# A convolution layer's second projection by seven block products instead of eight, with sums made by adding DMA transfers

## The chip, the cores and the metric

The kernel runs on one core of a Trainium2 chip. The metric is the device time in microseconds (us) of one execution. The chip's TensorE is called PE in what follows, VectorE DVE, ScalarE ACT, GpSimd POOL and SyncE SP, as in the profile's pages; PEld is PE's loading of weights. SP and POOL issue the DMA transfers of the part that matters here.

## The reference

Two decoder layers on x of 1024 tokens by 1024 channels, all in float32. Layer 0 has a short convolution as its token mixer, layer 1 attention in a window of 128; each is followed by a SwiGLU channel mixer.

```python
def short_conv_mixer(h, w_in, conv_w, w_out):
    b_gate, c_gate, xv = jnp.split(h @ w_in, 3, axis=-1)
    u = b_gate * xv
    y = lax.conv_general_dilated(u, conv_w[:, None, :], ...)   # causal, width 3, one filter per channel
    return (c_gate * y) @ w_out                                 # the second projection: 1024 x 1024

def swiglu_ffn(h, w_gate_up, w_down):
    g, u = jnp.split(h @ w_gate_up, 2, axis=-1)
    return (jax.nn.silu(g) * u) @ w_down

for i in range(2):
    h = rmsnorm(x, norm_mixer[i])
    x = x + (short_conv_mixer(h, ...) if i == 0 else swa_sink_attention(h, ...))
    h = rmsnorm(x, norm_ffn[i])
    x = x + swiglu_ffn(h, w_gate_up[i], w_down[i])
```

## The kernel before

Everything is kept transposed: a tile `X0` to `X7` holds 128 channels by 1024 tokens, and a half of it (`lo_half`, `hi_half`) is 512 tokens. To keep float32 accuracy every operand and every weight is split into a high and a low part, `hi` (a cast on ACT) and `lo` (the rest, by a subtraction on DVE, `split_steps`). One product of a 128x128 weight block with 512 tokens is then three matmuls: hi by hi, hi by lo, lo by hi.

Most of the large products are block products of two by two blocks with seven products in place of eight (a Winograd form). The four operand blocks are an even and an odd channel tile, each by the two halves of the tokens. Seven sums of operands (kinds `k` = 0 to 6, `put` splits them) meet seven sums of weights. One product of such a kind, called a unit here, goes over four pairs of channel tiles: 4 x 3 = 12 matmuls. Results of several kinds accumulate in one PSUM bank (`acc`, four of them, or `P0`, `P1`).

Four of the seven weight operands are sums of weight blocks. `sums_in_place`, `store_sums` and `weight_sums` make them: SP loads raw blocks, DVE adds and subtracts, POOL stores the sums to DRAM, and SP loads them again when a unit wants them. The operand sums (T1 to T4, `sum_t1` to `sum_t4`) are made by DVE as well.

The second projection `w_out` of the convolution does not work so before. It is the "tail" of `channel_mixer`: for each half `h` and each of the eight output tiles `m`, `tail_item` runs 8 x 3 = 24 matmuls over the eight tiles `z` of the gated convolution (`split_z`), with weights that `tail_weights` loads and splits. Then DVE adds the residual tile `X[m]`, which `load_again` has fetched from DRAM, ACT squares the result, POOL stores it (`xres`), and DVE adds the square to the running sum `s0` or `s1` (`L1054`, `L1058`). While the tail runs, weights of the channel mixer's first three kinds are loaded, split and kept (`early`), and its weight sums are made.

When a half is complete, `half_chain` follows: PE sums the squares over the channels (`mean`, L1071), DVE and ACT make the inverse root (`guess`), and PE turns it into rows (`turn`, L1083). DVE then multiplies the eight tiles by gain and rows (`scale`, L1093), and `put` splits them into the channel mixer's operands.

The order on every engine is written out by hand. A `Line` has work on PE, one piece behind another, each matmul counted as 0.2265 (`MM`), and `at(t, f)` issues `f` on its engine just ahead of the PE work that stands at time `t` of that plan. Each engine runs its queue in that order, so an instruction that has to wait holds up all that stand behind it on its engine. A granule of weights (`ring_granule`) is planned so: its load 20 us ahead of its matmuls, its hi 13 us, its lo 12.2 us ahead. Eight buffers `G` form the ring for split weights, `WR` and `WH` hold raw ones.

In the plan, `s` is the place at which `lead_in` begins: there the convolution's last unit products and the second projection meet. `begin1` and `begin2` are the ends of the projection's first and second half.

Of the kernel before, what the change touches and what calls it, by code (L numbers as in the profile page):

```python
# [83 lines left out]
def trunk_kernel(ctx: ExitStack, tc: tile.TileContext, xT, small, w_in, w_out, w_qk, w_v, w_o, w_gu, w_dn, out):  # L84
# [212 lines left out]
    def conv_layer():  # L297
# [80 lines left out]

        at(-7.6, mean)
# [126 lines left out]
        def gate(j, h, src):  # L506
            c = halves[h]
            dve.tensor_tensor(Y[j][:, c], src(), Y[j][:, c], ALU.mult)
# [163 lines left out]
        def gate_back(j, name):  # L672
            dve.tensor_tensor(Y[j], R[name], Y[j], ALU.mult)
# [13 lines left out]
        z = [None] * NK  # L687

        def split_z(j, tag, h, t):
            it = {}  # L690

            def hi():
                if z[j] is None:
                    z[j] = pair_slot(tag)
                it["steps"] = split_steps(z[j][:, 0, halves[h]], z[j][:, 1, halves[h]], Y[j][:, halves[h]])
                it["steps"][0]()

            at(t, hi)
            at(t + 0.7, lambda: it["steps"][1]())

        def load_again(m, t):
            def load():
                X[m] = slot(f"X{m}")
                load_x(m)

            at(t, load)

        def lead_in(part):
            u = n_units - 1
            s = line.end  # L710
            for k in (2, 5, 3):
                steady(u, k)
            part(0, 0, range(4))
            steady(u, 4)
            part(0, 1, range(4))
            steady(u, 6)
            tags = ("A0", "A1", "A2", "A3", "A4", "A5", "XS4", "XS5")
            e = line.end - s
            low = (-6.5, -5.5, 0.2, 1.2, 5.6, 6.6, 8.6, e - 2 * unit + 0.8)
            high = (-1.5, 8.0, 10.0, e - 1.0, e + 4.0, e + 9.0, e + 14.0, e + 19.0)  # L720
            again = (1.0, 10.0, 12.0, e + 3.5, e + 7.0, e + 12.0, e + 17.0, e + 22.0)
            for j in range(NK):
                split_z(j, tags[j], 0, s + low[j])
                split_z(j, tags[j], 1, s + high[j])
                load_again(j, s + again[j])
            return {(0, 0): 4, (0, 1): 4}
# [4 lines left out]
            lambda m: w_out[m],  # L731
            z,
            raw_tags=("XS0", "XS1", "XS2", "XS3"),
            extra_tags=("XS6", "XS7"),
            keep_tags=None,
            line=line,
            lead_in=lead_in,
            slots=(
# [10 lines left out]

    xres = [tc.dram_tile((P, T), F32, name=f"xres{m}") for m in range(NK)]  # L750
    first_sums = [[tc.dram_tile((4, P, 4 * P), F32, name=f"s1_{l}_{u}") for u in range(GROUP)] for l in range(2)]
    down_sums = [[tc.dram_tile((4, P, PAIRS * P), F32, name=f"s2_{l}_{u}") for u in range(GROUP)] for l in range(2)]
# [41 lines left out]
    def weight_sums(dst, w1, w2, j0, n, raw_tag, sum_tag, line=None, t=0.0):  # L794

        c = slice(j0 * P, (j0 + n) * P)
        it = {}

        def load():
            raw = slot(raw_tag, (P, 2, 2, 2 * P), bufs=2 if raw_tag == "WL" else 1)[:, :, :, 0 : n * P]  # L800
            nc.sync.dma_start(raw[:, 0], w1[:, :, c])
            nc.sync.dma_start(raw[:, 1], w2[:, :, c])
            it["raw"] = raw

        def add():
            raw = it["raw"]
            s = it["s"] = slot(sum_tag, (P, 4, 2 * P), bufs=2 if sum_tag == "WL" else 1)[:, :, 0 : n * P]
            for f in sums_of(raw[:, 0, 0], raw[:, 0, 1], raw[:, 1, 0], raw[:, 1, 1], s[:, 3], s[:, 0], s[:, 2], s[:, 1]):
                f()

        def store():
            nc.gpsimd.dma_start(dst[:, :, c].rearrange("s p c -> p s c"), it["s"])

        if line is None:
            load()
            add()
            store()
        else:
            line.at(t, load)
            line.at(t + 7.0, add)  # L820
            line.at(t + 9.5, store)
# [27 lines left out]
    def scheme(line, ring_tags):  # L849
# [22 lines left out]
        ring = deque(ring_tags)  # L872
# [5 lines left out]
        raws = {"n": 0}  # L878
# [48 lines left out]
        def bank_at(u, name, tag):  # L927
# [10 lines left out]
            ring=ring,  # L938
            ring_room=ring_room,
# [7 lines left out]
    def operands_of(line, slots):  # L947

        B = {k: [] for k in range(KINDS)}

        def put(k, p, src, t, lo_eng=dve):
            it = {}

            def hi():
# [3 lines left out]
                it["steps"] = split_steps(o[:, 0, :], o[:, 1, :], src(), lo_eng)  # L958
# [7 lines left out]
    def channel_mixer(layer, next_stage, src_of, operands, raw_tags, extra_tags, keep_tags, slots, begin_with=(), first_w=None, line=None, lead_in=None):  # L966
# [9 lines left out]
        tools = scheme(line, [f"G{(3 + i) % RING}" for i in range(RING)])  # L976
# [62 lines left out]

        def tail_item(h, m, k0=0):  # L1040
# [3 lines left out]
            t = line.end  # L1044

            def square():
                if m == 0:
# [6 lines left out]
            at(t + 0.05, lambda: dve.tensor_tensor(X[m][:, c], get(), X[m][:, c], ALU.add))  # L1054
            at(t + 0.8, square)
            at(t + 0.9, lambda: nc.gpsimd.dma_start(xres[m][:, c], X[m][:, c]))
            if m:
# [37 lines left out]
        first_items = {}  # L1095
        if lead_in is not None:
            first_items = lead_in(tail_part)
        origin = line.end - sum(first_items.values()) * 3 * MM
        begin1 = origin + 8 * tail
        begin2 = origin + 16 * tail  # L1100
        for h in (0, 1):
            for m in range(NK):
                tail_item(h, m, first_items.get((h, m), 0))
# [3 lines left out]
        extra_rooms = rooms(extra_tags)  # L1107
        pairs = [{} for u in range(GROUP)]
        whole = len(raw_tags) == GROUP

        def first_raw(u, k):
            if k < 2:
                return pairs[u]["raw"][:, 0, k]
            return pairs[u]["raw"][:, 1, 1] if whole else pairs[0]["s2"][:, u]
# [7 lines left out]
        def load_s2():  # L1122
            pairs[0]["s2"] = slot(raw_tags[0], (P, 4, 4 * P))
            for u in range(GROUP):
                nc.sync.dma_start(pairs[0]["s2"][:, u], first_sums[layer][u][SUMS[2]])


        for u in range(GROUP):
            if whole:
                t = (origin + 4.0, origin + 12.0, begin1 + 1.0, begin1 + 8.0)[u]  # L1130
                at(t, load_pair, pairs[u], raw_tags[u], w_gu[layer, u], w_gu[layer, NF + u])
                ts = (t + 8.0, t + 10.0, t + 18.0)
                at(t + 12.0, sums_in_place, pairs[u], 0)
                at(t + 14.0, sums_in_place, pairs[u], 2)
                at(t + 15.5, store_sums, pairs[u], first_sums[layer][u])
            else:
                at(origin + 1.0 + u, load_first, u)
                ts = [origin + 8 * tail * f for f in (0.28 + 0.14 * u, 0.35 + 0.14 * u, 0.9 + 0.07 * u)]
            for k in range(3):
                split_granule(early[k, u], lambda u=u, k=k: first_raw(u, k), 4, extra_rooms[u] if k == 2 else ring_room, ts[k])  # L1140
# [1013 lines left out]
```

## Time and profile before

| | |
|---|---|
| median of three runs | 1940.71 us (1940.19 to 1941.73) |
| profiled execution | 1941.99 us, of which its span is 1940.0 us |
| PE, PEld, busy | 1933.7 us (100%), 1617.8 us (83%) |
| DVE, ACT, POOL busy | 1363.7 us (70%), 864.8 us (45%), 247.4 us (13%) |
| granted PE clock | 0.999 |
| DMA | 311.75 MB, mean 161 GB/s |

The span runs from the first instruction to the last, and the time of an execution has about 2 us around it. Busy shares are means over stages that differ; what an engine waits for is read from the views of the trace. A matmul's busy time overlaps with that of the next, so PE's pace is read from the starts of its matmuls.

### The profile page before, as it was taken

How to read it: one execution, taken by the hardware profiler on the slowest of the kernel's cores; microseconds unless marked ns; L12 is line 12 of the kernel's file. 1: busy time of each engine (PE TensorE's matmuls, PEld its weight loads, DVE VectorE, ACT ScalarE, POOL GpSimd, SP SyncE). 2: the span in 40 equal slices, each digit the busy share in tenths (PEclk: the TensorE clock that was granted, in tenths of full speed). 3: DMA queues.
4: the chain of work that ended last, by engine and by line, in shares of the span. 5: the costliest groups of instructions: out<-in, count | busy, mean ns of one | idle time of the engine just before them, and what ended most of it. 6: DMA issues, size and time to landing. Idle time of an engine off the chain costs nothing.

```text
span 1940.0 us, 25506 instructions
## 1 busy us (share of the span) xinstructions
PE 1933.7 (100%) x9153; PEld 1617.8 (83%) x9153; DVE 1363.7 (70%) x2432; ACT 864.8 (45%) x1702; POOL 247.4 (13%) x350
## 2 busy tenths in 40 slices
PE   9999999999999999999999999999999999999999
PEld 7888888888888888888898888888888888888887
DVE  8998767876777676765744777788677766775543
ACT  5543434523333335444435887656233333344441
POOL 0000011011111110000003445310111111110000
PEclk9999999999999999999999999999999999999999
DMA  8532285244565448976300000152455455378562
GB/s 320 162 98 88 65 305 183 82 158 174 184 202 177 175 159 284 332 268 200 119 23 23 23 12 17 37 192 63 161 195 183 171 199 179 134 272 288 190 231 101
DMA packets 143167, 311.75 MB, mean 161 GB/s; under 512 B 13888, under 2 KB 53952, under 8 KB 143040
## 3 DMA queue, kind: packets, MB, share of 16 engines
q1 hardware_dynamic: 118992, 225.67, 35.3%
q0 software_dynamic: 23904, 84.42, 11.2%
q8 instruction: 72, 1.18, 0.3%
q14 instruction: 55, 0.45, 0.1%
q10 hardware_dynamic: 144, 0.03, 0.0%
HBM read 219.36 MB, written 90.70 MB: 160 GB/s over the span
## 4 chain that ended last, share of the span: by engine, by line
PE 96%; DVE 2%; DMA 1%; issue 1%; ACT 0%; DVEq 0%; ACTq 0%
PE acc L906 15%; PE acc L909 15%; PE acc L907 15%; PE P L906 9%; PE P L907 9%; PE P L909 9%; PE acc L167 7%; PE acc L171 3%; PE acc L1036 2%; PE acc L1034 2%; PE acc L1035 2%; PE P L1779 1%; PE P L1603 1%; PE P L1804 1%; PE P L1805 1%; PE P L1737 1%
## 5 line engine op out<-in xcount | busy, mean ns | idle before, releaser
L906 PE MATMUL acc<-XS,G 128*128 128x512 f32 x894 | 348.2, 389 | 0.0
L909 PE MATMUL acc<-XS,G 128*128 128x512 f32 x894 | 347.8, 389 | 0.0
L907 PE MATMUL acc<-XS,G 128*128 128x512 f32 x894 | 347.8, 389 | 0.0
L909 PEld LDWEIGHTS acc<-XS,G 128*128 128x128 f32 x894 | 167.8, 188 | 34.9
L907 PEld LDWEIGHTS acc<-XS,G 128*128 128x128 f32 x894 | 167.8, 188 | 34.8
L906 PEld LDWEIGHTS acc<-XS,G 128*128 128x128 f32 x894 | 167.8, 188 | 34.8
L906 PE MATMUL P<-A,G 128*128 128x512 f32 x502 | 195.3, 389 | 0.0
L907 PE MATMUL P<-A,G 128*128 128x512 f32 x502 | 195.3, 389 | 0.0
L909 PE MATMUL P<-A,G 128*128 128x512 f32 x502 | 195.3, 389 | 0.0
L906 PE MATMUL acc<-A,G 128*128 128x512 f32 x410 | 159.5, 389 | 0.0
L907 PE MATMUL acc<-A,G 128*128 128x512 f32 x410 | 159.5, 389 | 0.0
L909 PE MATMUL acc<-A,G 128*128 128x512 f32 x410 | 159.5, 389 | 0.0
L846 DVE TENSOR_TENSOR G<-WL,G 128x512 fp32r<-128x512 f32 x168 | 115.0, 685 | 52.9 <-ACT G L845 52.9
L167 PE MATMUL acc<-XS,WH 128*128 128x512 f32 x480 | 148.6, 409 | 0.8 <-ACT WH L139 0.7
L845 ACT CAST G<-WR 128x512 fp32r<-128x512 f32 (+1 forms) x198 | 119.6, 604 | 63.3 <-PE acc L909 25.6
L846 DVE TENSOR_TENSOR G<-WR,G 128x512 fp32r<-128x512 f32 (+1 forms) x198 | 132.0, 667 | 10.9 <-ACT G L845 10.6
L845 ACT CAST G<-WH 128x512 fp32r<-128x512 f32 (+1 forms) x156 | 93.7, 600 | 81.5 <-PE acc L909 42.1
L1206 ACT ACTIVATE G<-G 128x512 f32<-128x512 f32 x88 | 55.7, 634 | 161.7 <-DVE G L1277 157.6
L845 ACT CAST G<-WL 128x512 fp32r<-128x512 f32 x168 | 103.6, 616 | 37.0 <-DVE WL L789 33.2
L906 PE MATMUL P<-XS,G 128*128 128x512 f32 x290 | 112.9, 389 | 0.1
L909 PE MATMUL P<-XS,G 128*128 128x512 f32 x290 | 112.8, 389 | 0.0
L907 PE MATMUL P<-XS,G 128*128 128x512 f32 x290 | 112.8, 389 | 0.0
(320 smaller groups left out, 3884.2 us busy)
## 6 DMA issues: line engine op xcount, KB each, us to landing
G<-h SPq DMA_DIRECT2D x70, 512.0 KB, 5.3
h<-X POOLq DMA_DIRECT2D x44, 512.0 KB, 5.7
X<-in_w_dn SPq DMA_DIRECT2D x80, 256.0 KB, 3.5
s<-X POOLq DMA_DIRECT2D x40, 512.0 KB, 4.5
WR<-in_w_gu SPq DMA_DIRECT2D x36, 512.0 KB, 5.7
WH<-in_w_gu SPq DMA_DIRECT2D x36, 512.0 KB, 6.1
h<-X POOLq DMA_DIRECT2D x66, 256.0 KB, 4.3
WR<-s SPq DMA_DIRECT2D x52, 256.0 KB, 3.3
```

Of the source, the lines that this page charges most:

```text
L167: pe.matmul(ps.half(h), wh, xs[:, j, c], start=first and j == 0, stop=False)
L171: pe.matmul(ps.half(h), wl, xs[:, 0, c], start=False, stop=last)
L845: lambda: act.copy(out_hi, raw),
L846: lambda: lo_eng.tensor_tensor(out_lo, raw, plain(out_hi), ALU.subtract),
L906: pe.matmul(ps, w[:, 0, c], x[:, 0, :], start=start and e == 0, stop=False, skip_group_check=True)
L907: pe.matmul(ps, w[:, 0, c], x[:, 1, :], start=False, stop=False, skip_group_check=True)
L909: pe.matmul(ps, w[:, 1, c], x[:, 0, :], start=False, stop=last, skip_group_check=True)
L1034: pe.matmul(ps, hi[:, kc], xs[:, 0, c], start=k == 0, stop=False, skip_group_check=True)
L1035: pe.matmul(ps, hi[:, kc], xs[:, 1, c], start=False, stop=False, skip_group_check=True)
L1036: pe.matmul(ps, lo[:, kc], xs[:, 0, c], start=False, stop=k == n_op - 1, skip_group_check=True)
L1206: state["silu"] = act.activation(x, x, AF.Silu)
L1603: pe.transpose(pb[:, t], wide[:, t], ident)
```

## The change

The second projection now uses the seven products too. `out_product(u, k)` is a unit of 12 matmuls for a pair of output tiles `u` (four pairs), so 7 x 4 units take the place of 2 x 8 items; the weights go through the ring. `lead_in` orders everything around it. Kinds 0 and 1 and kinds 2 to 4 of the units share a bank, and results are added to `X[m]` with the sign that the kind asks for.

Three kinds of sums are made by DMA transfers that add to what their target holds (`accum_op=ALU.add`, issued by POOL): the weight sums (`added_sums`: SP copies the four blocks from DRAM to DRAM, then POOL issues four adding transfers) for `w_out`, for the channel mixers' first group and for `w_down`; the operand sums of z for three of the four pairs of tiles (`add_by_dma`; the fourth is added by DVE, `add_here`); and the residual for three quarters of the output (`copy_out`: ACT copies the bank to `X[m]`, POOL adds x from DRAM to it). For transfers can only add, the signs of the operands change: some are split with a minus (`split_steps_of_minus`, `gate`), and results are subtracted in their place. The weights of the first three kinds of layer 0's channel mixer are no longer kept early: they come through the ring, each 20 us ahead of its use.

```diff
+        out_sums = tc.dram_tile((4, GROUP, P, 5 * P), F32, name="s3")
+        for u in (0, 2):
+            dst = [out_sums[i, u : u + 2][:, :, 0 : 4 * P] for i in range(4)]
+            parts = [w_out[2 * u + r : 2 * u + 4 : 2][:, :, c] for r in (0, 1) for c in (0, 1)]
+            added_sums(dst, parts, line, 60.0 + 9.0 * u, 18.0)
+        first_added_sums(0, line, 120.0, 18.0)
...
+        def out_product(u, k):
+            srcs = {0: w_out[2 * u][:, 0], 1: w_out[2 * u][:, 1], 4: w_out[2 * u + 1][:, 1]}
+            src = srcs[k] if k in srcs else out_sums[SUMS[k], u][:, 0 : 4 * P]
+            name = {1: "d1", 5: "e", 6: "e"}.get(k, "d")
+            tag = "acc" if k in (0, 2, 3, 4) else f"P{u % 2}" if k == 1 or u < 2 else "acc"
+            get = bank_at(("out", u), name, tag)
+            ring_granule(4, lambda: Z[k], 0, get, k in (0, 1, 5), True, src=src)
...
         def lead_in(done):
             s = line.end
+            def add_by_dma(to, of):
+                nc.gpsimd.dma_start(to(), of(), accum_op=ALU.add)
...
+                k0, k1, k2, k3, k4, k5, k6 = (
+                    (-7.6, 0.3, 7.0, 11.0, 27.4, 4.6, 36.0),
+                    (-6.5, 1.0, 9.8, 12.4, 28.5, 5.7, 37.1),
...
+                if p < 3:
+                    t_1, t_c, t_2, t_3, t_4 = ((-4.4, 0.2, 1.6, 3.6, 8.2), (-3.5, 1.2, 2.6, 4.5, 9.2), (-2.6, 7.6, 9.4, 5.4, 15.0))[p]
+                    at(s + t_1, add_by_dma, b11, b12)
+                    at(s + t_c, lambda t2=t2, b22=b22: act.copy(t2(), b22()))
+                    at(s + t_2, add_by_dma, t2, b11)
+                    at(s + t_3, add_by_dma, b12, b22)
+                    at(s + t_4, add_by_dma, b21, t2)
...
+                put_z(2, p, t2, s + k2)
...
+            def copy_out(get, m, h, t, sign):
+                c = halves[h]
+                at(t, lambda: act.activation(X[m][:, c], get(), AF.Copy, scale=sign))
+                at(t + 0.9, lambda: nc.gpsimd.dma_start(X[m][:, c], x_of(m, h), accum_op=ALU.add))
+
+            def add_out(get, m, h, t, op):
+                c = halves[h]
+                at(t, lambda: dve.tensor_tensor(X[m][:, c], X[m][:, c], get(), op))
...
             for k in (2, 5, 3):
+                steady(v, k)
+            for u in (0, 1):
+                first[u] = out_product(u, 0)
+            steady(v, 4)
+            first[2] = out_product(2, 0)
+            steady(v, 6)
+            first[3] = out_product(3, 0)
+            for k in range(1, KINDS):
+                for u in range(GROUP):
+                    get, m, h = out_product(u, k)
+                    t = line.end
+                    if k == 1:
+                        copy_out(*first[u], t - 7.0, 1.0)
+                    if k in (2, 3):
+                        copy_out(get, m, h, t + 0.05, 1.0 if k == 2 else -1.0)
+                    else:
+                        add_out(get, m, h, t + 0.05, ALU.subtract if k in (4, 6) else ALU.add)
+                        done(h, m, t)
+                if k == 4:
+                    begin1 = line.end
+            return begin1, line.end
...
+    def added_sums(dst, parts, line, t, gap):
+        def copy(i):
+            nc.sync.dma_start(dst[i], parts[i])
+        def add(to, of):
+            nc.gpsimd.dma_start(dst[to], dst[of], accum_op=ALU.add)
+        for i in range(4):
+            line.at(t + 0.5 * gap * i, copy, i)
+        for i, (to, of) in enumerate(((0, 2), (2, 3), (3, 0), (1, 3))):
+            line.at(t + gap * (2.5 + i), add, to, of)
...
-        pieces = [(m, j, min(2, PAIRS - j)) for j in range(0, PAIRS, 2) for m in range(GROUP)]
...
+        for m in range(GROUP):
+            dst = [down_sums[layer][m][i][:, 0 : PAIRS * P] for i in range(4)]
+            parts = [w_dn[layer, 2 * m + r][:, c] for r in (0, 1) for c in (0, 1)]
+            added_sums(dst, parts, line, steady_begins + 75.0 * m, 9.0)
+        if layer == 0:
+            first_added_sums(1, line, begin + 10.0, 18.0)
```

What moves on the engines, as the built programs have it (a name carries its buffer's number and its own). On PE, at the change from one output bank of the projection to the next, before:

```order
L1036 MATMUL acc_322_2177<-XS4_309_2065,WL_318_2142 128x512
L1034 MATMUL acc_322_2177<-XS5_314_2109,WH_317_2141 128x512
L1035 MATMUL acc_322_2177<-XS5_314_2109,WH_317_2141 128x512
L1036 MATMUL acc_322_2177<-XS5_314_2109,WL_318_2142 128x512
L1034 MATMUL acc_331_2228<-A0_289_1941,WH_323_2182 128x512
```

and the same place now, where weights come from the ring's `G` buffers:

```order
L992 MATMUL acc_313_2111<-A1_291_1959,G1_293_1981 128x512
L993 MATMUL acc_313_2111<-A1_291_1959,G1_293_1981 128x512
L995 MATMUL acc_313_2111<-A1_291_1959,G1_293_1981 128x512
L992 MATMUL acc_317_2140<-A0_290_1958,G2_297_2010 128x512
L993 MATMUL acc_317_2140<-A0_290_1958,G2_297_2010 128x512
```

The projection's rows are 576 - 192 = 384 matmuls before (the lines L1034 to L1036 have 576 rows, 192 of them in layer 1) and 28 x 12 = 336 now, and the whole program has 8637 rows on PE before and 8589 now: 48 fewer.

On DVE, the rows just ahead of the second half's chain, whose first row is the `TENSOR_SCALAR` on `hr_m`. `s1` is the running sum of squares that PE's `mean` reads. Before:

```order
L1093 SCALAR_TENSOR_TENSOR X7_349_2332<-X7_349_2332,cst_1_61,P2_375_2499 128x512
L846 TENSOR_TENSOR XS3_406_2704<-X7_349_2332,XS3_406_2704 128x512
L1054 TENSOR_TENSOR X6_343_2289<-acc_407_2725,X6_343_2289 128x512
L1058 TENSOR_TENSOR s1_376_2508<-s1_376_2508,G10_412_2773 128x512
L1054 TENSOR_TENSOR X7_349_2332<-acc_411_2765,X7_349_2332 128x512
L1058 TENSOR_TENSOR s1_376_2508<-s1_376_2508,G11_414_2803 128x512
L1076 TENSOR_SCALAR hr_m_418_2827<-P3_417_2822 128x4
```

and now:

```order
L1189 SCALAR_TENSOR_TENSOR X5_237_1542<-X5_237_1542,cst_1_61,P2_392_2682 128x512
L926 TENSOR_TENSOR G4_413_2821<-WR_404_2756,G4_413_2821 128x512
L1154 TENSOR_TENSOR s1_385_2650<-s1_385_2650,G10_414_2826 128x512
L926 TENSOR_TENSOR XS3_409_2788<-X5_237_1542,XS3_409_2788 128x512
L1189 SCALAR_TENSOR_TENSOR X7_295_1996<-X7_295_1996,cst_1_61,P2_392_2682 128x512
L781 TENSOR_TENSOR X6_275_1845<-X6_275_1845,acc_398_2710 128x512
L926 TENSOR_TENSOR G5_417_2847<-WH_407_2782,G5_417_2847 128x512
L926 TENSOR_TENSOR XS3_409_2788<-X7_295_1996,XS3_409_2788 128x512
L1154 TENSOR_TENSOR s1_385_2650<-s1_385_2650,G10_418_2853 128x512
L1172 TENSOR_SCALAR hr_m_424_2883<-P3_423_2878 128x4
```

The last scaling of the first half (`X7`), the last splits (`XS3`) and the ring's splits (`G4`, `G5`) now stand among the second half's last adds, close ahead of the last `s1`; between `begin1` and `begin2` lie 8 units (kinds 5 and 6) where 8 items of 24 matmuls lay.

On ACT, shortly behind `s`, with the semaphores that each row waits for. `XS2` is kind 2's operand, `WL_298` the sum T2 that two adding transfers make (`DMASW`: a transfer issued by POOL), and the `COPY` to `s1_314` empties the bank of the convolution's last unit:

```order
L925 CAST A4_306_2078<-X0_253_1653 128x512 [waits DMASW7_49,PE_49]
L925 CAST A4_306_2078<-X2_197_1218 128x512 [waits DMASW0_49]
L925 CAST G0_308_2090<-WL_280_1892 128x512
L925 CAST XS2_309_2100<-WL_298_2028 128x512 [waits DMASW2_49]
L756 COPY WL_312_2108<-X5_237_1542 128x512 [waits DVE_49]
L571 COPY s1_314_2116<-acc_285_1931 128x512 [waits PE_49]
L925 CAST A5_307_2079<-X4_220_1404 128x512 [waits DMASW1_49]
L925 CAST G3_315_2119<-WH_302_2050 128x512 [waits DMAHW1_49]
```

Before, the rows around the same copy wait for PE, for DVE and for loads of SP, and for no transfer of POOL:

```order
L845 CAST A4_303_2040<-X4_220_1400 128x512 [waits PE_49]
L845 CAST A5_304_2046<-X5_237_1535 128x512 [waits PE_49]
L845 CAST A1_291_1949<-X1_195_1196 128x512
L562 COPY s1_306_2060<-acc_284_1908 128x512 [waits PE_49]
L845 CAST WH_307_2062<-WR_295_1989 128x1024 [waits DMAHW7_49,DVE_49]
```

Four waits for adding transfers now stand in ACT's queue around the copy of that bank.

More of the change, by code (lines that the diff above doesn't have):

```diff
@@ L708, in lead_in @@
-        def lead_in(part):
-            u = n_units - 1
-            s = line.end
-            for k in (2, 5, 3):
[L712 to L726, printed above, removed]
+        Z, put_z = operands_of(
+            line,
+            {
+                0: ("A0", "A1"),
+                1: ("A2", "A3"),
+                2: ("XS2", "XS3"),
+                3: ("XS4", "XS5"),
+                4: ("A0", "A1"),
+                5: ("A4", "A5"),
+                6: ("A2", "A3"),
+            },
+        )
@@ L737, in conv_layer @@
             lead_in=lead_in,
+            before=tools,
             slots=(
@@ L792, in sums_of, with pure_sums_of, first_added_sums @@
         ]
[L794 to L821, printed above, removed]
+    def pure_sums_of(a11, a12, a21, a22, s2, s3, s1, s4):
+        return [
+            lambda: dve.tensor_tensor(s3, a11, a21, ALU.add),
+            lambda: dve.tensor_tensor(s2, a22, s3, ALU.add),
+            lambda: dve.tensor_tensor(s4, a12, s2, ALU.add),
+            lambda: dve.tensor_tensor(s1, a21, a22, ALU.add),
+        ]
+    def added_sums(dst, parts, line, t, gap):
[7 more added lines that the diff above has]
+            line.at(t + gap * (2.5 + i), add, to, of)
+    def first_added_sums(layer, line, t, gap):
+        tile_ = first_sums[layer]
+        for u in (0, 2):
+            dst = [tile_[i, u : u + 2][:, :, 0 : 4 * P] for i in range(4)]
+            parts = [w_gu[layer, r * NF + u : r * NF + u + 2][:, :, c] for r, c in ((0, 0), (0, 1), (1, 0), (1, 1))]
+            added_sums(dst, parts, line, t + 0.5 * u * gap, gap)
     def load_pair(it, tag, w1, w2):
@@ L847, in split_steps, with split_steps_of_minus, scheme @@
         )
-    def scheme(line, ring_tags):
+    def split_steps_of_minus(out_hi, out_lo, raw, lo_eng=dve):
+        return (
+            lambda: act.activation(out_hi, raw, AF.Copy, scale=-1.0),
+            lambda: lo_eng.scalar_tensor_tensor(out_lo, raw, -1.0, plain(out_hi), ALU.mult, ALU.subtract),
+        )
+    def scheme(line, ring_tags, before=None):
         at = line.at
@@ L870, in rooms @@
             return out_
-        ring = deque(ring_tags)
+        ring = before.ring if before else deque(ring_tags)
         def ring_room():
@@ L974, in channel_mixer @@
         unit = 12 * MM
-        tools = scheme(line, [f"G{(3 + i) % RING}" for i in range(RING)])
+        tools = scheme(line, [f"G{(3 + i) % RING}" for i in range(RING)], before)
         units, rooms, ring, ring_room = tools.units, tools.rooms, tools.ring, tools.ring_room
@@ L1044, in tail_item, with tail_done @@
             t = line.end
+            at(t + 0.05, lambda: dve.tensor_tensor(X[m][:, c], get(), X[m][:, c], ALU.add))
+            tail_done(h, m, t)
+        def tail_done(h, m, t):
+            c = slice(h * HALF, h * HALF + HALF)
+            first = h not in begun
+            begun.add(h)
             def square():
-                if m == 0:
+                if first:
                     state["ss", h] = slot(f"s{h}", (P, HALF))
```

179 lines of the change are left out of this document (93 added, 86 removed).

## The prediction

> **What bounds the kernel now.** I read the page first, its busy shares and its row of PE clocks; then the waits of PE, summed by line; then the timelines of PE and DVE around the second projection.
>
> ```profile
> span 1940.0 us, 25506 instructions
> PE 1933.7 (100%) x9153; PEld 1617.8 (83%) x9153; DVE 1363.7 (70%) x2432; ACT 864.8 (45%) x1702; POOL 247.4 (13%) x350
> PEclk9999999999999999999999999999999999999999
> PE 96%; DVE 2%; DMA 1%; issue 1%; ACT 0%; DVEq 0%; ACTq 0%
> ```
>
> PE is busy for all but 6.3 us of the span, its clock is granted nearly in full in every slice, and the chain that ended last is PE for 96%. So the time is the number of matmuls by the pace of one, plus whatever PE waits. The waits of PE on other engines (in all, times, longest) are these two:
>
> ```profile
> PE P L323 <- DVE s L320: 1.5, 1, 1.5
> PE acc L167 <- ACT WH L139: 0.7, 1, 0.7
> ```
>
> Both lie outside the part that is changed. DVE, ACT and POOL cost nothing as long as they keep ahead of PE; the question is what the change saves on PE and whether the other engines then still keep ahead.
>
> The pace of the large products, from two rows of PE's timeline in the convolution mixer (start, busy time):
>
> ```profile
> 191.23 0.39 PE L906 MATMUL acc<-XS,G 128*128 128x512 f32 x1
> 204.83 0.39 PE L906 MATMUL P<-XS,G 128*128 128x512 f32 x1
> ```
>
> Between them PE starts 60 matmuls (five units of 12): 13.60 / 60 = 0.2267 us each. The 0.39 in the row is one matmul from start to end, and overlaps its neighbours.
>
> **What the change removes on PE.** 384 matmuls become 336, and nothing else changes PE's count: 48 fewer. As all of PE's time is on the path, 48 x 0.2267 = 10.9 us go. The projection before runs in one unbroken row at the same pace, as the two means in PE's timeline show, the first matmuls of each half's chain:
>
> ```profile
> 290.51 0.95 PE L1071 MATMUL P<-cst,s 128*128 128x1 f32 x8
> 335.85 0.92 PE L1071 MATMUL P<-cst,s 128*128 128x1 f32 x7
> ```
>
> Between them lie 8 items of 24 = 192 matmuls, 43.5 us, in 45.3 us: 1.8 us are the mean, the turn and small gaps. No wait of PE on DVE is in it.
>
> **What it adds: DVE is late for the second mean.** Now 96 matmuls (8 units of 12) lie between the means, not 192. PE arrives at the second mean 96 x 0.2267 + 1.8 = 23.6 us after the first. The mean reads `s1`, and DVE's queue puts 36 operations between the first half's first scaling of `X0` and the last add to `s1`, both counted: 28 of the `TENSOR_TENSOR` sort and 8 scalings (`SCALAR_TENSOR_TENSOR`). DVE is in order, so the mean waits for all of them. Rows of DVE's timeline, for the lag from mean to scaling and for the pace (what ended an idle time stands in brackets):
>
> ```profile
> 294.14 0.75 DVE L1093 SCALAR_TENSOR_TENSOR X<-X,cst,P 128x512 f32<-128x512 f32 x1 [0.44 <-PE P L1083]
> 298.95 0.69 DVE L1054 TENSOR_TENSOR X<-acc,X 128x512 f32<-128x512 f32 x1 [0.28 <-PE acc L1036]
> 299.56 0.74 DVE L1093 SCALAR_TENSOR_TENSOR X<-X,cst,P 128x512 f32<-128x512 f32 x1
> 300.22 0.68 DVE L846 TENSOR_TENSOR G<-XS,G 128x512 fp32r<-128x512 f32 x1
> 301.95 0.68 DVE L1058 TENSOR_TENSOR s<-s,G 128x512 f32<-128x512 f32 x1
> 302.56 0.68 DVE L846 TENSOR_TENSOR XS<-X,XS 128x512 fp32r<-128x512 f32 x1
> 336.81 0.16 DVE L1076 TENSOR_SCALAR hr_m<-P 128x4 f32<-128x4 f32 x1 [2.72 <-PE P L1071]
> ```
>
> The first scaling starts 294.14 - 290.51 = 3.6 us after the mean does. From start to start an add takes 0.61 (298.95 to 299.56, and 301.95 to 302.56) and a scaling 0.66. So DVE needs 28 x 0.605 + 8 x 0.665 = 22.3 us, and I allow 0.4 for short waits on ACT: the last add to `s1` ends 3.6 + 22.3 + 0.4 = 26.3 us after the first mean. PE waits 26.3 - 23.6 = 2.7 us. Before, there is slack instead: in the last row DVE had been idle for 2.72 us when the mean's result came. The cost has bounds: 0 if DVE finds 2.7 us that I don't see, 5 if ACT, whose squares stand between DVE's adds, is late by some 0.6 for each of four.
>
> **Then DVE is late for the first bank of the channel mixer.** Behind the second mean DVE scales eight tiles again, and among the scalings stand the adds that empty `P0` and `P1`, which the channel mixer's first group takes again. `P0` is wanted after 55 matmuls, 55 x 0.2267 + 1.8 = 14.3 us behind the mean; DVE reaches it after 6 scalings and 10 adds, 3.6 + 4.0 + 6.1 + 0.4 = 14.1: no wait. `P1` is wanted after 67 matmuls, 17.0; DVE has 7 scalings and 15 adds to do, 3.6 + 4.7 + 9.1 + 0.4 = 17.8, some 0.8 us late. I take 0.7, between 0 and 2 (the operation after it would be late by as much).
>
> **What costs nothing, and by what cover.** Subtracting for adding, and splitting with a minus, change the form of an operation and not the count; the scaling's row above against the add's shows a second form 0.06 us dearer, off PE's path. DVE loses its weight sums, but PE never waited for them, so this earns nothing. The weights that were kept early now come through the ring with 20 us of lead; a load takes some 3.3 to 5.7 us by these rows of the issues (KB each, median us to landing), so the cover is over 10 us:
>
> ```profile
> G<-h SPq DMA_DIRECT2D x70, 512.0 KB, 5.3
> h<-X POOLq DMA_DIRECT2D x44, 512.0 KB, 5.7
> s<-X POOLq DMA_DIRECT2D x40, 512.0 KB, 4.5
> h<-X POOLq DMA_DIRECT2D x66, 256.0 KB, 4.3
> WR<-s SPq DMA_DIRECT2D x52, 256.0 KB, 3.3
> xres<-X POOLq DMA_DIRECT2D x32, 256.0 KB, 3.4
> X<-xres SPq DMA_DIRECT2D x16, 512.0 KB, 7.4
> ```
>
> **The adding transfers** are the one operation that no row of before shows. An add of 256 KB can't be told cheaper than a plain store of 256 KB, 3.4 us; as it reads its target too, it moves what a 512 KB transfer moves, 4.5 to 7.4. I take 5, near the middle of these, with 3.4 and 7.4 as the ends. Call an add's latency D. The tightest place is the first pair's T2: the add into `b11` is issued at s - 4.4, the one into `t2` at s + 1.6, or when the first has landed; kind 2's cast on ACT stands at s + 7.0. Behind it on ACT stands the copy of the bank of the convolution's last unit, which PE wants after five units, 5 x 12 x 0.2267 = 13.6. With D = 5 the second add lands at s + 6.6, ahead of the cast. With D over 6 it lands at 2D - 4.4, and with three ACT operations of 0.6 behind it PE waits from D = 8.1 on, and then by 2D - 16.1 us. All ends of my range lie below. The residual's adds for `P0` are issued at about s + 21.1 and DVE wants them at s + 27.3, PE the bank at s + 29.9; free up to about D = 7, late by 0.4 at 7.4. The sums of weights in DRAM have 9 to 18 us between their adds, and are loaded tens of us later. So the adds cost 0 here.
>
> The Trainium skill's page "Collectives: The Full Stack", section "The bandwidth ceiling: the fold count and why AG ≠ RS ≠ AR", says that an adding transfer runs at half the rate of a copy, since each add reads two sources. That doubles the bytes as above and speaks for 5.7 rather than 3.4; the sum is the same by the one and the other, and no run so far shows an adding transfer.
>
> **The sum.** -10.9 + 2.7 + 0.7 = -7.5 us. The profiled execution of before took 1941.99 (span 1940.0), 1.28 over the median of 1940.71; the same kernel would profile at 1934.5 with a span of 1932.5, and the median is 1940.7 - 7.5 = **1933.2**. Measurements of this kernel tell about 0.2%, 3.9 us, from no change: faster is below 1936.8, slower above 1944.6.
>
> **Rivals.**
> 1. *The full gain.* DVE keeps up after all, since ring splits stand in its queue later than they run, or its waits are shorter. Then 1940.7 - 10.9 = 1929.8. For it: DVE needs only a tenth less. Against: its queue is in order, and its pace in the rows is a steady one. Chance 0.15.
> 2. *The pause costs clock too.* A longer pause of PE before the second mean, and matmuls at a lower clock behind it. The kernel's start shows what such matmuls cost, nine in a row behind an idle PE:
>
> ```profile
> 1.46 3.71 PE L323 MATMUL P<-s 128*128 128x512 f32 x9 [1.46 <-DVE s L320]
> ```
>
> 3.71 / 9 = 0.41 us against 0.2267. Eight to nine matmuls at that pace lose 9 x 0.18 = 1.7 us: 1934.9, or up to 1936.8 if DVE is late as well by the upper bound. Against it: the clock row shows no dip before, and a wait of 2.7 us is short. Chance 0.08. The Trainium skill's page "TensorE: Matmul & The Clock Gate", Part 1, has the clock halved after an idle window of some 3.4 us; by that rule my 2.7 us stay free of it and the upper bound of 5 does not; no wait in this trace is long enough to show it.
> 3. *Adds or loads somewhat late.* Adds with D from 9.9 to 13.7, or loads pushed back by the new copies from DRAM to DRAM (the DMA engines have digits of 5 to 9 in the page around the projection), add 3.6 to 11.4 us (2D - 16.1): 1936.8 to 1944.6. For it: POOL issues stores, sums and residuals in one queue. Chance 0.13.
> 4. *Slower: adds of 14 us or more hold ACT.* From D = 13.8 on, kind 2's cast waits for T2, and the copy behind it on ACT holds the bank, by 2D - 16.1 = 11.5 us or more: 1933.2 + 11.5 = 1944.7 and up; at D = 20 it is 1957. For it: the add's price is not in the trace, and four such waits stand on ACT around the copy. Against: this is twice the slowest 512 KB row. A change that adds nothing to PE and does not take the 48 matmuls away is excluded by the count of its rows. Chance 0.14.
>
> **How the numbers follow.** The forecast, PE's count less DVE's lateness between 0.7 and 7 us, has 0.50: 1930.5 to 1936.8. With rivals 1 and 2 faster has 0.73, rival 3 is the same with 0.13, rival 4 slower with 0.14. The range from 1929.5 (the full gain) to 1941.0 (adds of D = 12, 7.8 us late) leaves out rival 4, the upper part of rival 3 and little below.
>
> **What would show it.** In the trace after: PE with 48 fewer matmul rows at 0.2267 us; in PE's waits a new row on DVE's `s` at the mean, some 2.7 us once, and one on DVE for a `P` bank of the channel mixer, under 2 us; PE's clock row unchanged; adding transfers of 256 KB landing in 3.4 to 7.4 us; no row of PE on ACT for the bank at `s`. Wrong would be: no wait at the second mean (rival 1), adds over 8 us with PE waiting on ACT or POOL (rivals 3, 4), or a wait elsewhere that I have not named.

## The result and the profile after

The changed kernel takes 1982.51 us (1982.40 to 1984.59) where the kernel before takes 1940.58: a ratio of 1.0216 (95% interval 1.0204 to 1.0229), 42 us slower and not 7.5 faster. The profiled execution took 1982.42, its span 1980.6, 40.6 more than before. First the page of the changed kernel (the engines' busy times, the clock row, the chain):

```profile
span 1980.6 us, 25183 instructions
PE 1929.6 (97%) x9105; PEld 1612.1 (81%) x9105; DVE 1285.6 (65%) x2222; ACT 876.7 (44%) x1741; POOL 272.9 (14%) x370
PEclk9997999999999999999999999999999999999999
PE 85%; DVE 5%; DMA 5%; issue 3%; ACT 1%; POOL 1%; POOLq 0%; ACTq 0%; DVEq 0%
```

PE has its 48 matmul rows fewer, but it is no longer the whole chain, and one slice has lost clock. Then the waits of PE (in all, times, longest):

```profile
PE acc L992 <- ACT G L555: 18.9, 1, 18.9
PE P L992 <- DVE G L543: 14.1, 1, 14.1
PE P L992 <- DVE X L781: 7.0, 1, 7.0
PE P L1167 <- DVE s L1154: 3.5, 1, 3.5
PE P L992 <- DVE G L1328: 1.2, 2, 0.8
```

The last two of these rows are the two that were forecast (the second mean, and a `P` bank of the channel mixer); the third is the residual's bank `P0`. The first two lie in the convolution mixer, some 70 us and more ahead of the part where I looked. What precedes the first shows in PE's timeline, ACT's, and SP's (for SP, how long issuing took), from the moment when the copies of `w_out` start:

```profile
134.11 0.39 PE L995 MATMUL P<-A,G 128*128 128x512 f32 x1
153.38 0.80 PE L992 MATMUL acc<-XS,G 128*128 128x512 f32 x1 [18.87 <-ACT G L555]
153.97 0.63 PE L993 MATMUL acc<-XS,G 128*128 128x512 f32 x1
154.40 0.63 PE L995 MATMUL acc<-XS,G 128*128 128x512 f32 x1
156.53 0.46 PE L993 MATMUL acc<-XS,G 128*128 128x512 f32 x1
156.82 0.39 PE L995 MATMUL acc<-XS,G 128*128 128x512 f32 x1
```

```profile
151.61 0.62 ACT L925 CAST G<-WR 128x512 fp32r<-128x512 f32 x1 [19.43 <-DMA WR<-in_w_in]
152.13 0.72 ACT L501 ACTIVATE X<-G,cst 128x512 f32<-128x512 f32 x1
152.76 0.56 ACT L555 COPY G<-acc 128x512 f32<-128x512 f32 x1
```

```profile
99.73 0.77 SPq L886 DMA_DIRECT2D s<-in_w_out  x1
109.87 19.13 SPq L886 DMA_DIRECT2D s<-in_w_out  x3
129.12 10.02 SPq L629 DMA_DIRECT2D WR<-in_w_in  x1
141.11 23.47 SPq L886 DMA_DIRECT2D s<-in_w_out  x3
164.69 11.23 SPq L629 DMA_DIRECT2D WR<-in_w_in  x1
```

ACT's cast waits 19.4 us for a load of `w_in`; the copy that empties PE's bank stands behind it. SP is held for 19 us in issuing three copies, and for 10 in issuing the load behind them. DMA is not busy meanwhile, as the windows show (length; busy time of PE, PEld, DVE, ACT, POOL; clock; DMA share; GB/s), here 12 us of it:

```profile
125.00:137.00 12.00, 9.50 (x42) 7.52 (x41) 7.88 (x12) 3.17 (x6) 0.00 (x0) 1.00 0.13 51
```

A share of 0.13 is what two of 16 engines make when they work all the time. The PE rows above give the rest of the bill: behind the gap matmuls start 0.43 apart and not 0.2267 (153.97 to 154.40), since PE's clock is granted by half there. Of the eight starts until the pace is back, the first comes 0.59 behind the one before it, six come 0.43 and the last 0.29: 0.36 + 6 x 0.2 + 0.06 = some 1.6 us are lost. All four long waits of this kernel, 3.5 to 18.9 us, are followed by such a stretch. So the span's 40.6 are: -10.9 for PE's count, 18.9 + 14.1 + 7.0 + 3.5 + 1.2 = 44.7 of new waits, and 4 x 1.6 = 6.4 of half clock, 40.2 together.

### The profile page after: what moved, and what is told of

Read it like the earlier page. It is cut to its first block, busy times and chain, and to the rows that moved or that the text cites. A ratio compares the mean times of both kernels' runs of the same rounds, so it can differ in the third digit from the quotient of the medians.

```text
span 1980.6 us, 25183 instructions
## 1 busy us (share of the span) xinstructions
PE 1929.6 (97%) x9105; PEld 1612.1 (81%) x9105; DVE 1285.6 (65%) x2222; ACT 876.7 (44%) x1741; POOL 272.9 (14%) x370
## 4 chain that ended last, share of the span: by engine, by line
PE 85%; DVE 5%; DMA 5%; issue 3%; ACT 1%; POOL 1%; POOLq 0%; ACTq 0%; DVEq 0%
PE acc L992 14%; PE acc L993 14%; PE acc L995 14%; PE P L992 8%; PE P L993 8%; PE P L995 8%; PE acc L167 6%; DMA WR<-in_w_in 4%; PE acc L171 3%; PE P L1857 1%; DVE G L926 1%; PE P L1681 1%; PE P L1882 1%; PE acc L1122 1%; PE acc L1124 1%
## 5 line engine op out<-in xcount | busy, mean ns | idle before, releaser
L992 PE MATMUL acc<-XS,G 128*128 128x512 f32 x942 | 368.5, 391 | 18.9 <-ACT G L555 18.9
L993 PE MATMUL acc<-XS,G 128*128 128x512 f32 x942 | 367.6, 390 | 0.0
L995 PE MATMUL acc<-XS,G 128*128 128x512 f32 x942 | 367.4, 390 | 0.0
L992 PE MATMUL P<-A,G 128*128 128x512 f32 x534 | 209.7, 393 | 21.2 <-DVE G L543 14.1
L992 PEld LDWEIGHTS acc<-XS,G 128*128 128x128 f32 x942 | 177.6, 189 | 56.2 <-ACT G L555 19.3
L993 PE MATMUL P<-A,G 128*128 128x512 f32 x534 | 208.8, 391 | 0.0
L995 PE MATMUL P<-A,G 128*128 128x512 f32 x534 | 208.7, 391 | 0.0
L995 PEld LDWEIGHTS acc<-XS,G 128*128 128x128 f32 x942 | 177.6, 189 | 37.2
L993 PEld LDWEIGHTS acc<-XS,G 128*128 128x128 f32 x942 | 177.7, 189 | 36.7
L926 DVE TENSOR_TENSOR G<-WR,G 128x512 fp32r<-128x512 f32 (+1 forms) x218 | 145.8, 669 | 70.0 <-ACT G L925 69.4
L925 ACT CAST G<-WR 128x512 fp32r<-128x512 f32 (+1 forms) x218 | 131.8, 605 | 111.5 <-DMA WR<-in_w_in 49.4
L992 PE MATMUL acc<-A,G 128*128 128x512 f32 x458 | 178.3, 389 | 0.0
L995 PE MATMUL acc<-A,G 128*128 128x512 f32 x458 | 178.2, 389 | 0.0
L993 PE MATMUL acc<-A,G 128*128 128x512 f32 x458 | 178.2, 389 | 0.0
L925 ACT CAST G<-WH 128x512 fp32r<-128x512 f32 (+1 forms) x176 | 105.9, 602 | 87.4 <-PE acc L995 43.2
L992 PEld LDWEIGHTS P<-A,G 128*128 128x128 f32 x534 | 101.0, 189 | 43.5 <-DVE G L543 15.0
L926 DVE TENSOR_TENSOR G<-WH,G 128x512 fp32r<-128x512 f32 (+1 forms) x176 | 116.9, 664 | 20.2 <-ACT G L925 20.1
L995 PEld LDWEIGHTS P<-A,G 128*128 128x128 f32 x534 | 100.9, 189 | 21.2
```

Of the source, the lines that this page charges most:

```text
L925: lambda: act.copy(out_hi, raw),
L926: lambda: lo_eng.tensor_tensor(out_lo, raw, plain(out_hi), ALU.subtract),
L992: pe.matmul(ps, w[:, 0, c], x[:, 0, :], start=start and e == 0, stop=False, skip_group_check=True)
L993: pe.matmul(ps, w[:, 0, c], x[:, 1, :], start=False, stop=False, skip_group_check=True)
L995: pe.matmul(ps, w[:, 1, c], x[:, 0, :], start=False, stop=last, skip_group_check=True)
```

## The experiments

Theory A: `out_sums[i, u:u+2]` from `w_out[2*u+r : 2*u+4 : 2]` is a transfer whose outermost dimension is two tiles that don't adjoin; it runs on two DMA engines, and what stands behind it in SP's queue waits. Its rivals: copies from DRAM to DRAM crowd the engines whatever their shape (B), or POOL's adding transfers are what is slow (C). The edits below are shortened to what they change.

**Rows first, in the changed kernel.**

```diff
-            nc.sync.dma_start(dst[i], parts[i])
+            nc.sync.dma_start(dst[i].rearrange("u p c -> p u c"), parts[i].rearrange("u p c -> p u c"))   # w_out's eight copies
```

> The changed kernel with one difference: the eight copies of w_out from DRAM to DRAM run with the 128 rows as the outermost dimension instead of the two tiles (same bytes, same rows of 2 KB, same place in the queue). Theory A (with the two tiles outermost each copy runs on two of the 16 DMA engines, takes over 10 us, and holds the loads queued behind it on SP): the waits of 18.9 and 14.1 us and the half-clock matmuls behind them go, some 36 us; the 7.0 us wait at 303 us goes too if it came from the same delay: 1937 to 1947. Theory B (copies from DRAM to DRAM crowd the DMA engines in this stage, whatever their shape): 1975 to 1985. Theory C (the adding transfers on POOL are what is slow): 1975 to 1985.

1947.89 us, ratio to before 1.0029 (1.0018 to 1.0040): some 35 of the 42 us are gone by the order of two dimensions. The waits of PE in its trace:

```profile
PE P L998 <- DVE X L785: 8.2, 1, 8.2
PE P L1173 <- DVE s L1160: 3.5, 1, 3.5
PE P L998 <- DVE G L1334: 1.2, 2, 0.8
```

Both waits in the convolution mixer are gone; the residual's bank remains, so that wait has a cause of its own.

**The copies alone, in the kernel before**, into a tensor that nobody reads, with two tiles outermost, and with the rows outermost.

```diff
+        copies = tc.dram_tile((4, GROUP, P, 5 * P), F32, name="copies")
+        for u in (0, 2):
+            for i, (o, c) in enumerate(((0, 0), (0, 1), (1, 0), (1, 1))):
+                to, of = copies[i, u : u + 2][:, :, 0 : 4 * P], w_out[2 * u + o : 2 * u + 4 : 2][...]
+                line.at(60.0 + 9.0 * u + 9.0 * i, lambda to=to, of=of: nc.sync.dma_start(to, of))
```

> The kernel before, with eight copies of w_out from DRAM to DRAM added to SP's queue at the places and with the two tiles outermost as in the changed kernel, into a tensor that nobody reads; no adding transfers, no other change. Theories A and B: 25 to 40 us slower than before, 1966 to 1981, with PE waits at the same two places of the convolution mixer. Theory C: no change, 1939 to 1943.

> As the run before it, but the copies with the 128 rows outermost. Theory A: no change, 1939 to 1943. Theory B: 25 to 40 us slower, 1966 to 1981. Theory C: no change.

1973.37 us (1.0162, 1.0147 to 1.0178) with two tiles outermost, 1941.70 (1.0002, 0.9992 to 1.0011) with the rows outermost. The first shows waits at the same two places as the changed kernel:

```profile
PE acc L911 <- ACT G L551: 16.1, 1, 16.1
PE P L911 <- DVE G L539: 10.0, 1, 10.0
```

So the copies are enough without any adding transfer, and their bytes do no harm in the other shape: A holds, B and C fall. The two waits are 6.9 us shorter in all than the changed kernel's 33.0; what else in the change lengthens them there is not shown.

**Four and eight outermost**, the same bytes in the same rows of 2 KB, in the kernel before. `to` and `of` are 4 tiles x 64 rows (`w_out[o:8:2]`) or 8 tiles x 32 rows (`w_out[0:8]`) of 512 columns.

```diff
-                to, of = copies[i, u : u + 2][:, :, 0 : 4 * P], w_out[2 * u + o : 2 * u + 4 : 2][...]
+                to, of = copies[j, 0:4, 0:64, 0 : 4 * P], w_out[o:8:2][:, row : row + 64, ...]
```

> The kernel before with the same eight copies of w_out added at the same places, 512 KB each in rows of 2 KB, but with an outermost dimension of four (tiles) and 64 rows in each. Theory A (as many DMA engines work as the outermost dimension has entries, up to 16): where only copies run, a DMA share of 0.25 and some 100 GB/s, a copy in 5 to 6 us, and the loads behind lag half as long: 1941 to 1950, against 1973 with two and 1942 with 128 outermost. If the non-adjoining tiles as such are slow, and not the number two: 1965 to 1980, and a share of 0.13.

> As the run before it, with an outermost dimension of eight tiles and 32 rows in each. Theory A: a DMA share of up to 0.5 where only copies run, some 200 GB/s, no waits of PE: 1940 to 1943.

1941.70 and 1941.69 us, ratios 1.0001 (0.9990 to 1.0012) and 0.9997 (0.9986 to 1.0009). Windows in which the copies run, for two, four, eight and 128 outermost in turn:

```profile
125.00:134.00 9.00, 9.00 (x42) 7.39 (x40) 7.65 (x12) 2.94 (x6) 0.00 (x0) 1.00 0.13 51
```

```profile
127.00:132.00 5.00, 5.00 (x24) 4.14 (x23) 4.67 (x8) 2.73 (x5) 0.00 (x0) 1.00 0.26 104
```

```profile
127.00:132.00 5.00, 5.00 (x23) 4.13 (x22) 4.67 (x8) 2.34 (x4) 0.00 (x0) 1.00 0.52 205
```

```profile
115.00:122.00 7.00, 7.00 (x32) 5.80 (x32) 6.50 (x12) 0.64 (x2) 0.00 (x0) 1.00 1.04 393
```

Share and rate double from row to row; the last, a share of 1.04, is all 16 engines. Four engines already suffice for PE: at 104 GB/s it waits for none of the loads. The Trainium skill's page "DMA: Bandwidth & Descriptors", section "Why a DMA increments its semaphore by 16 and not by 1", says that a transfer uses the largest number of engines, up to 16, that divides the slowest dimension of both sides; these four rows agree.

The two tiles of `w_out` don't adjoin (the slice has a step of 2). The changed kernel also copies `w_gu` in pairs of tiles, but of adjoining ones. How long one copy of each kind held SP (ns, least, median and most; first and last start):

```profile
L886 SPq DMA_DIRECT2D s<-in_w_out x8: 627/5102/11305, 99.7 to 178.8; - x8
L886 SPq DMA_DIRECT2D s<-in_w_gu x8: 496/548/1130, 193.3 to 232.6; - x8
```

A pair that adjoins does not hold SP so: two tiles alone don't make the slow shape.

**The copies on POOL's queue**, still two tiles outermost.

```diff
-            nc.sync.dma_start(dst[i], parts[i])
+            for r in range(0, P, 32):
+                nc.gpsimd.dma_start(dst[i][:, r : r + 32], parts[i][:, r : r + 32])
```

> The changed kernel with the w_out copies, still two tiles outermost, issued by POOL instead of SP, each in four pieces of 32 rows. If what hurts is that SP's loads stand in one queue behind the copies, most of the 36 us go: 1938 to 1950. If it is enough that two of the 16 engines are busy, since every load needs a part from each, the waits stay: 1970 to 1985.

2041.97 us (1.0515, 1.0498 to 1.0531), a miss for both branches. The waits in the convolution mixer are gone, as SP's queue predicts; but POOL needs some 5.7 us for each of 32 pieces, and the sums' and z's adds stand behind them (PE's wait, and the row of ACT that waits ahead of that copy):

```profile
PE acc L999 <- ACT s L576: 89.1, 1, 89.1
325.43 0.62 ACT L932 CAST A<-X 128x512 fp32r<-128x512 f32 x1 [90.60 <-DMA X<-X]
```

This is rival 4 of the prediction, at another price: late adds hold ACT, and ACT holds the bank. That the loads were spared doesn't say whether the queue or the busy engines held them before, since smaller pieces on POOL move at a lower rate than the copies on SP (128 KB in 5.7 us). The changed kernel's own trace says that each was enough. Its load behind the cast's wait of 19.4 us began to issue at 129.12. The same load in the kernel before:

```profile
112.41 0.33 SPq L620 DMA_DIRECT2D WR<-in_w_in  x1
```

There such loads landed in 3.4 us, and the first cast of this one started at 129.97, so it had 14.2 us to spare. In the changed kernel its issue began 16.7 us later, and the cast could start only 22.5 us after that, 19.1 more than 3.4. Either delay alone is more than 14.2.

**Why the residual's bank is late.** In the trace with the rows first, POOL issues two adds of weight sums, then z's last add, and then sits for 7.75 us, for nothing that the profile names, ahead of the residual's first:

```profile
246.82 0.94 POOL L895 DMA_DIRECT2D s<-s  x1 [3.27 <-issue]
253.45 0.89 POOL L895 DMA_DIRECT2D s<-s  x1 [5.68 <-issue]
254.02 1.22 POOL L735 DMA_DIRECT2D X<-WL  x1
263.00 2.69 POOL L781 DMA_DIRECT2D X<-in_xT  x3 [7.75 <-issue]
```

The add issued at 253.45 took 9.2 us to land, so the stall ends 0.3 us behind its landing. Theory R: POOL waits for room for the descriptors of its transfers, and gets it when that add is through. One edit gives more room, another takes the weight sums out of the way.

```diff
-    nc = bacc.Bacc("TRN2", target_bir_lowering=False, num_devices=1, dynamic_dma_scratch_size=1024)
+    nc = bacc.Bacc("TRN2", target_bir_lowering=False, num_devices=1, dynamic_dma_scratch_size=1280)
```

```diff
-        first_added_sums(0, line, 120.0, 18.0)
+        first_added_sums(0, line, 66.0, 18.0)
```

> The kernel with the copies' rows first, and 1280 instead of 1024 bytes for the descriptors of POOL's transfers; nothing else. Theory R (POOL's 7.75 us wait ahead of the residual's first add is for room among its descriptors, taken by an add of 512 KB of weight sums): the first residual add, on X0, issues right behind the add before it, near 255 to 256 us instead of 263, the 8.2 us wait of PE for P0 goes, and a wait for the second bank, P1, of up to 6 us takes its place, since the room ends one add later: 1944 to 1948. Theory L (the residual's adds are late by their own landing of some 6 us, or wait for something else): the issue stays at 263 and the wait at 8 us.

> The kernel with the copies' rows first, and the weight sums of the channel mixer's first group (copies and adds) started 54 us earlier in the plan, at 66 instead of 120, so that none of their adds stands among those of z and of the residual. Theory R: PE's wait of 8.2 us for P0 and the half-clock matmuls behind it go (10 us): 1936 to 1940. Theory L: the wait stays between 6 and 9 us: 1946 to 1949.

More room: 1939.95 us in one run, beside 1941.17 for the kernel before. The residual's first add goes out behind z's last:

```profile
253.03 0.89 POOL L735 DMA_DIRECT2D X<-WL  x1 [4.71 <-issue]
253.63 1.19 POOL L781 DMA_DIRECT2D X<-in_xT  x1
```

PE's wait there falls from 8.2 to 2.5 in two pieces, with no half clock behind them. That is better than the 1944 to 1948 that I expected, and R holds. Earlier sums: 1951.97 us (1.0059, 1.0042 to 1.0075), a miss. The wait for `P0` did go, but sixteen adds, some 6 us each one behind the other on POOL, now reach into z's:

```profile
226.11 0.89 POOL L895 DMA_DIRECT2D s<-s  x1 [5.21 <-issue]
231.99 0.90 POOL L895 DMA_DIRECT2D s<-s  x1 [4.99 <-DVE X L519]
```

PE waits 4.5 and 3.6 us for z's operands and banks instead, in the fastest of four runs (1947.54).

**DVE and the second mean** (on top of the rows first):

```diff
                 t += 2 * pace
+            t += 5.0        # behind the first four of the first half's scalings
```

> The kernel with the copies' rows first, and the first half's last four scalings with their splits 5 us later in the plan, so that some six DVE operations move from ahead of the second mean to behind it. Theory Q (the second mean waits because DVE has too much queued ahead of the last add to s1): the wait of 3.5 us goes, and with it the half-clock matmuls behind it (1.8 us): 1942 to 1945. If the lateness only moves to the channel mixer's first bank: 1946 to 1949, with a longer wait of PE for P there.

1946.11 us (1.0026, 1.0015 to 1.0037), not to be told in time from the run without it, and in the range that was expected if the lateness only moves. The waits show both:

```profile
PE P L1185 <- DVE X L1195: 2.4, 2, 1.7
PE P L1173 <- DVE s L1160: 0.6, 1, 0.6
```

The mean waits 0.6 and not 3.5, but the turn behind it now waits 2.4, as it writes the bank `P2` that the delayed scalings still read. A run with the earlier sums as well:

> Copies with rows first, weight sums earlier and scalings later, all three. Theories A, R and Q together: PE's count of 48 matmuls fewer less about 1 us of waits, 1930 to 1935, faster than the kernel before. If R or Q is wrong, 4 to 10 us more.

1947.86 us (1.0038, 1.0023 to 1.0053): the waits for z from the earlier sums remain (4.5 and 2.5), a miss through the earlier sums, and not through A.

**Put together.** Rows first, room of 1344, the later scalings, the second half's rows in `P3`; then also all sums of weights early enough.

```diff
-                units["rows", h] = bank("P2")
+                units["rows", h] = bank(("P2", "P3")[h])
```

```diff
-            added_sums(dst, parts, line, 60.0 + 9.0 * u, 18.0)
+            added_sums(dst, parts, line, 36.0 + 9.0 * u, 18.0, copy)
-        first_added_sums(0, line, 120.0, 18.0)
+        first_added_sums(0, line, 56.0, 18.0)
```

> Copies with rows first, room of 1344 bytes for the descriptors of POOL's transfers, the first half's last scalings 5 us later, and the second half's rows in bank P3 instead of P2, so that the turn needn't wait for the scalings that still read P2. Theories A, R and Q together: against the 1940 of the kernel with more room alone, the second mean's wait of 3.5 us, the half-clock matmuls behind it (1.8 us) and some of the 2.5 us for the residual's banks go: 1933 to 1937. If DVE's lateness only moves to the channel mixer's banks: 1938 to 1941.

> As the run before it, with all weight sums started earlier in the plan (w_out's at 36 and 54, the first group's at 56), so that their sixteen adds, some 6 us each one behind the other on POOL, are through before z's. The waits for the residual's banks go altogether: 1931 to 1935. If the early copies crowd the loads of the convolution mixer, or the adds still reach into z's: 1936 to 1950.

The first takes 1939.50 us (0.9987, 0.9978 to 0.9996), a miss: it lies where it was expected if DVE's lateness only moves, and PE still waits 2.1 for a residual bank and 2.0 for a channel mixer's bank. The second takes 1935.83 (0.9972, 0.9960 to 0.9983), faster than both kernels and 0.8 above the range expected. What is left of the new waits on PE:

```profile
PE P L998 <- DVE G L1335: 2.8, 2, 2.0
PE P L1173 <- DVE s L1160: 0.6, 1, 0.6
```

Of the 10.9 us, 2.8 go to the channel mixer's first banks and 0.6 to the mean.

## Why the prediction was wrong

- **PE's count**, -10.9: right in its size. It shows once the new waits are gone: 1935.83 against 1941.76 in the same comparison, 5.9 faster with 3.4 of waits left. The last 1.6 have no cause that the runs show; half clock is not one, as the granted clock of that profiled run is 1.0.
- **The second mean**, +2.7: the mechanism was right, the term mis-sized. The last add to `s1` came 26.7 us after the first mean (26.3 worked out), PE waited 3.5. The wait also cost clock, some 1.7 us, which was rival 2, at its price; the upper end of that rival should read 1933.2 + 1.7 + (5 - 2.7) = 1937.2 and not 1936.8. The Trainium skill's page "TensorE: Matmul & The Clock Gate", Part 1, puts the idle window at some 3.4 us and calls it free-running; the last section's rows agree on both, and show that such a window need not be idle throughout. I had set my 2.7 against that length as if the wait's length alone decided.
- **The channel mixer's `P` bank**, +0.7: measured 1.2, in two pieces.
- **"The residual's adds ... late by 0.4 at 7.4"**: a first step that failed. The adds landed in 5.9 us, inside the bounds; they were issued late, for POOL's room was taken. I had priced each add by its latency and set aside the queue in which the weight sums' adds stand ahead of them, though I had listed both. 7.0 us and some 1.6 of clock.
- **"What costs nothing, and by what cover"**: the step that failed and that decided. The lead of 20 us over loads of 3.3 to 5.7 us was taken from rows in which every transfer has one side in SBUF, with its 128 rows outermost. The eight new copies got no term of their own; their bytes stood in rival 3 as a crowd, never the shape of one, and I had looked for effects around the projection, while the copies are issued up to 130 us earlier, among the convolution mixer's loads. In their place the runs showed copies at 51 GB/s that held loads of `w_in`: 33.0 us of waits and 3.2 of clock; with the rows first both waits are gone.
- **The adding transfers' latency** was within its bounds at the median:

```profile
X<-X POOLq DMA_DIRECT2D x6, 256.0 KB, 4.5
WL<-X POOLq DMA_DIRECT2D x3, 256.0 KB, 4.3
X<-in_xT POOLq DMA_DIRECT2D x12, 256.0 KB, 5.9
```

Single adds were not: z's last took 10.4 us, and one of the weight sums' 12.5. But PE has no wait for z or for the bank at `s` among its rows, which is what rivals 3 and 4 priced. So rival 4 had the sign and the wrong cause; the copies on POOL show its mechanism.

## What to carry to other kernels

For every transfer that a change adds, read the shape that is left when adjoining tiles and rows are taken as one dimension, and cost it by the engines that its outermost dimension occupies; then ask what stands behind it in its queue, also far from where its result is used. A DMA share of 0.13 with a waiting queue was such a transfer here, and not an idle DMA. A PE wait has two prices, its length and the half-clock matmuls behind it: some 1.6 us behind each long wait of the changed kernel, and 2.9 behind the wait of 4.5 with the earlier sums (13 starts 0.43 or more apart). Where a wait of 2 us or more is forecast, the second belongs in the range.

## What was not expected of the hardware

Two-tile copies ran at 51 GB/s, and at 104, 205 and 393 with four, eight and 128 outermost. Adds of 512 KB on POOL follow each other at some 6 us each, and raising the room for descriptors from 1024 to 1280 bytes took some 7 us off the kernel's time, in one run.

The clock does not follow a wait's length alone. With the earlier sums, matmuls behind a wait of 3.57 us start at the full pace; with room and later scalings a wait of 1.97 us is followed, 1.6 us on, by matmuls 0.43 apart. PE's rows of the two:

```profile
246.58 0.50 PE L998 MATMUL acc<-XS,G 128*128 128x512 f32 x1 [3.57 <-ACT s L575]
344.27 0.50 PE L998 MATMUL P<-XS,G 128*128 128x512 f32 x1 [1.97 <-DVE G L1335]
```

What decides shows when the span is cut where the granted clock changes. The half-clock stretches of the changed kernel last 17.07, 13.65, 6.83 and 3.41 us, which are five, four, two and one times 3.41. So the clock is set for one window of 3.41 us after the other, and these windows don't start with a pause. The windows around the two waits, the first run's counted back from its half clock at 258.59 (length; busy time of PE; clock; DMA share; GB/s):

```profile
241.53:244.94 3.41, 1.49 (x7) 1.00 1.03 186
244.94:248.35 3.41, 1.77 (x8) 1.00 1.06 191
```

```profile
342.25:345.66 3.41, 1.45 (x7) 1.00 0.28 77
345.66:349.08 3.42, 3.42 (x10) 0.50 0.27 77
```

The wait of 3.57 us falls across two windows and leaves PE busy for 1.49 and 1.77 us of them; the one of 1.97 lies in a single window and leaves 1.45, and the next window has half the clock. So among windows of such large matmuls the border lies near 1.5 us of work in 3.41. Matmuls of one column, as the mean's, seem to count for less than their busy time: one window that holds eight of them had 1.54 us busy and was followed by half clock as well (more room, 329.69 to 333.10). How they count is open.
